# Feed-forward down projection as seven half-size products with weight sums from GpSimd, and a longer matmul time in the recorder's schedule

## The chip, the core and the metric

The kernel runs on one core of a Trainium2 chip. The metric is the device time of one launch in microseconds; three runs of the kernel before gave 1825.97 us as their median (1824.64 to 1826.08).

## What is computed

Two layers of a decoder trunk on 512 tokens of 1024 features, in float32. A layer mixes tokens (convolution, two attentions, gates, an output projection and a layer norm) and then applies a gated feed-forward with a second layer norm. The change lies in the feed-forward and its norm:

```python
def conv_ffn(x, w_up, conv_w, conv_b, w_down):        # w_up 1024 x 5632, w_down 2816 x 1024
    h = causal_dwconv(x @ w_up, conv_w) + conv_b
    a, u = jnp.split(h, 2, axis=-1)
    return (jax.nn.gelu(a, approximate=False) * u) @ w_down
...
x = layer_norm(ALPHA * x + ffn, ln2_g[l], ln2_b[l])
```

## The kernel before

Every float32 product is made of three TensorE matmuls in the replicated-float32 type (F32R): each operand is split into a rounded part (hi, a copy by ScalarE) and the rest (lo, a subtraction by VectorE or GpSimd), and `mm3` adds hi·hi, hi·lo and lo·hi into one PSUM bank. Weights come in units of 128 x 1024 words (512 KB): `unit` issues the load into a `raw` tile on SyncE's queue, makes `wh` on ScalarE and `wl` on VectorE (or GpSimd where `lo=G`). `raw`, `wh` and `wl` have three buffers each. Activations of the feed-forward live in tiles with the tag `big` (eleven buffers).

The up projection has 44 units for a layer (two for each of 22 blocks of 128 hidden features). One unit is 24 matmuls of 512 columns into one of three `mm` banks. `conv_ffn` then takes two banks to one block: an activation and two VectorE operations for each bank, a Gelu, a product `c[0]*c[1]`, and the split of that block into hi and lo (`hb`).

The down projection (`g_tok_norm` with the kind `w_dn`) has tokens on the partitions: for each half n of the 1024 output columns, four token tiles t of 128 have a bank each, and 11 units of two 128-row blocks go by. A unit is 4 x 2 x 3 = 24 matmuls. The last three units of a half are held together so that the token tiles end one after the other; in the second half their lo parts are made on GpSimd. Each ended bank is added to `ALPHA` times the residual (`r`), `bn_stats` follows, and after the second half `g_norm(t)` normalises tile t, writes it out and, in the first layer, transposes and splits it for the next layer. In the last layer the last token tile is done in two matmuls of 256 columns instead of one of 512, so that its first half can be read earlier.

Two clocks set the order. `Sched` runs generators and advances its clock `now` by a matmul time for each matmul and by the waits in the table `DLY`; this is the order of tracing. `Recorder.schedule` then list-schedules all recorded instructions over the five engines with the durations of `Recorder.cost`, an instruction traced earlier going first, and `issue` writes each engine's queue in that order. Both clocks take `n / 2.4 + 3` ns for a matmul of n columns. Each engine runs its queue in order. All instructions carry the line number of one helper (L421 before, L427 after), so that groups are told apart by tile names.

Of the kernel before, what the change touches and what calls it, by code (L numbers as in the profile page):

```python
# [10 lines left out]
F32 = mybir.dt.float32  # L11
# [6 lines left out]
NFF = D_FF // 128  # L18
# [22 lines left out]
def _block(inp, key):  # L41
# [23 lines left out]
    if kind == "w_dn":  # L65
        return _k_block(inp["ffn_w_down"][l], 2 * key[3], 2 * key[3] + 2, key[2] * 512, key[2] * 512 + 512)
# [31 lines left out]
def _smalls(inp, l):  # L98
    """Per-layer constants that sit on partitions: [128, .]"""
# [13 lines left out]
N_UNITS = 290  # L113
# time (ns) that the other engines take until the tensor engine can go on with what a step has made
# [22 lines left out]
def _rearrange(idx, pattern, known):  # L137
    """einops on the free dimensions (the partition dimension p stays first)"""
# [21 lines left out]
class RAP:  # L160
    """an access pattern of a recorded tile: where it lies, and how to get it from the real tile"""
# [45 lines left out]
class Recorder:  # L207
    # ns from the end of an instruction to the start of one that needs it
# [59 lines left out]
    def cost(eng, name, args, kw, op):  # L268
# [34 lines left out]
    def schedule(self):  # L303
        """list scheduling in order of tracing; slots of a tag are given in order of first use"""
# [27 lines left out]
        def slots(op):  # L332
            """None if the slots can be had now, else when (or inf)"""
# [98 lines left out]

class Event:
# [39 lines left out]
def trunk(ctx, tc, xT_d, x_d, w_d, cst_d, sm_d, w1_d, gb_d, out_d, order):  # L473
# [48 lines left out]
    def mm(o, a, b, start, stop):  # L522
        T.matmul(o, a, b, start=start, stop=stop)
# [10 lines left out]
    def mm3(o, ah, al, bh, bl, start, stop):  # L534
        mm(o, ah, bh, start, False)
        mm(o, ah, bl, False, False)
        mm(o, al, bh, False, stop)

# [12 lines left out]
    def unit(*key, parts=1, lo=None):  # L551
# [3 lines left out]
        if key[1] == "n_v":  # L555
            n = 280 * (key[2][1] - key[2][0])
        raw = sb.tile([128, 1024], F32, tag="raw", bufs=3, name=nm("raw"))
# [21 lines left out]
    def g_halves(x, evs, keys):  # L579
        """the first products of a phase, by token halves, as the norm before it delivers them"""  # L580
# [27 lines left out]
    def stack_q(z, a0, a1):  # L608
        """a0 = [hi of rows 0:64; their lo], a1 = [lo of rows 64:128; their hi]"""
# [7 lines left out]
    def stack_k(z, h0, h1, l0, l1):  # L617
        """h0 = [hi; hi] of rows 0:64, h1 of rows 64:128, l0, l1 the same of the lo parts"""
# [6 lines left out]
    def softmax(o, n, mx, sums):  # L625
        """exp((o + causal mask) / 8 - its row maximum), the row sums into sums; mx is left at minus the maximum"""
# [6 lines left out]
    def rsqrt(v, n, r=None, o=None):  # L633
        """(v + eps) ** -0.5"""
# [11 lines left out]
    def g_tok_norm(l, kind, nk, lhs, res_d, gi, last):  # L646
        """norm(ALPHA * x + lhs^T w): the next x (transposed and split, per token tile an event, and in DRAM)"""
        r, st = [], []
        for t in range(4):
# [4 lines left out]
            n = 4 if last and t == 3 else 2  # L654
# [613 lines left out]
```

## Time and profile before

| what | value |
|---|---|
| device time, median of three runs (lowest, highest) | 1825.97 us (1824.64, 1826.08) |
| the profiled execution: span from the first to the last instruction | 1823.5 us |
| PE busy | 1796.3 us (99%) |
| DVE, ACT, POOL busy | 1108.0, 777.7, 216.8 us |
| mean granted TensorE clock | 0.998 |
| mean DMA rate | 106 GB/s |

The profiled execution has no time of its own beside its span; the three runs lie 1.1 to 2.6 us above the span, which is what lies around it. PE, DVE, ACT, POOL and SP are TensorE, VectorE, ScalarE, GpSimd and SyncE. A busy PE is an engine with a matmul in flight; how fast it goes is read from the distance between matmuls. A matmul row names its PSUM tile first, then weights and data. In the page an idle time is that of the engine just before the instruction, with the instruction that ended it.

### The profile page before, as it was taken

The numbers are of one execution on the slowest core, as the hardware profiler recorded it, in microseconds if no ns is written. First come the engines' busy times: TensorE is split into PE (matmuls) and PEld (weight loads), VectorE is DVE, ScalarE is ACT, GpSimd is POOL, SyncE is SP. The second block draws the span as 40 slices with busy tenths as digits, with TensorE's granted clock in tenths as the row PEclk, the third lists the DMA queues.
The fourth block names the chain that finished last, engine by engine and source line by source line (L and its number), as shares of the span: only waits on it lengthen the run. The fifth ranks groups of instructions, "written<-read, shape, count | busy, mean of one in ns | idle before, by whom it ended". The sixth has DMA issues, their size and how long they took to land.

```text
span 1823.5 us, 23236 instructions
## 1 busy us (share of the span) xinstructions
PE 1796.3 (99%) x8794; PEld 1506.6 (83%) x8794; DVE 1108.0 (61%) x1987; ACT 777.7 (43%) x1340; POOL 216.8 (12%) x264
## 2 busy tenths in 40 slices
PE   8999999999999999999999999999999999999997
PEld 7788888888888888888887888888888888888886
DVE  6968968534457566643389688674344666566334
ACT  4548854422324444421244587553223244444211
POOL 1300123000021000000234001120000400000004
PEclk9999999999999999999999999999999999999999
DMA  6520243233234223423254203332333333234221
GB/s 220 153 90 24 60 133 95 91 104 126 96 105 153 100 92 104 139 95 103 93 166 132 76 25 96 101 104 83 108 133 97 123 127 99 98 104 138 94 93 70
DMA packets 60976, 193.36 MB, mean 106 GB/s; under 512 B 7680, under 2 KB 9824, under 8 KB 60736
## 3 DMA queue, kind: packets, MB, share of 16 engines
q1 hardware_dynamic: 49984, 167.01, 27.6%
q0 software_dynamic: 10880, 24.88, 5.4%
q8 instruction: 69, 1.13, 0.3%
q14 instruction: 43, 0.35, 0.1%
HBM read 171.93 MB, written 8.39 MB: 99 GB/s over the span
## 4 chain that ended last, share of the span: by engine, by line
PE 90%; DVE 6%; issue 1%; ACT 1%; POOL 1%; DMA 1%; SPq 0%; POOLq 0%; DVEq 0%; ACTq 0%
PE mm L421 72%; PE sc L421 8%; PE pv L421 6%; DVE tmp L421 4%; PE tp L421 3%; DVE wl L421 1%; DVE s L421 1%; POOL tmp L421 1%; ACT tmp L421 0%; DMA tmp<-in_xT_dram 0%; DVE xl L421 0%; POOL s L421 0%; DVE big L421 0%; ACT big L421 0%; DMA big<-big 0%
## 5 line engine op out<-in xcount | busy, mean ns | idle before, releaser
L421 PE MATMUL mm<-xh,wh 128*128 128x512 f32 (+1 forms) x1632 | 619.9, 381 | 9.0 <-ACT wh L421 5.2
L421 PE MATMUL mm<-xl,wh 128*128 128x512 f32 (+1 forms) x1632 | 619.9, 380 | 3.0 <-DVE xl L421 2.5
L421 PE MATMUL mm<-xh,wl 128*128 128x512 f32 (+1 forms) x1632 | 619.6, 380 | 0.2
L421 DVE TENSOR_TENSOR wl<-raw,wh 128x1024 fp32r<-128x1024 f32 (+2 forms) x270 | 331.8, 1230 | 437.7 <-ACT wh L421 433.6
L421 ACT ACTIVATE wh<-raw 128x1024 fp32r<-128x1024 f32 (+2 forms) x291 | 306.1, 1052 | 523.5 <-PE mm L421 336.4
L421 PEld LDWEIGHTS mm<-xh,wh 128*128 128x128 f32 x1632 | 308.0, 189 | 62.3 <-ACT wh L421 5.2
L421 PEld LDWEIGHTS mm<-xl,wh 128*128 128x128 f32 x1632 | 308.7, 189 | 57.1 <-DVE xl L421 4.5
L421 PEld LDWEIGHTS mm<-xh,wl 128*128 128x128 f32 x1632 | 308.3, 189 | 56.3 <-DVE wl L421 1.3
L421 PE MATMUL mm<-wh,big 128*128 128x512 f32 (+1 forms) x600 | 187.9, 382 | 0.0
L421 ACT ACTIVATE tmp<-tmp,s 128x512 f32<-128x512 f32 (+3 forms) x261 | 140.5, 558 | 63.5 <-DVE s L421 47.0
L421 DVE SCALAR_TENSOR_TENSOR tmp<-mm,smf,tmp 128x511 f32<-128x511 f32 (+1 forms) x176 | 131.3, 746 | 3.1
L421 PEld LDWEIGHTS mm<-wh,big 128*128 128x128 f32 x600 | 111.8, 188 | 21.9
L421 ACT ACTIVATE big<-tmp 128x512 fp32r<-128x512 f32 (+1 forms) x100 | 62.9, 629 | 142.9 <-DVE tmp L421 142.2
L421 PE MATMUL mm<-big,wh 128*128 128x512 f32 x384 | 120.2, 392 | 0.0
L421 PE MATMUL mm<-wl,big 128*128 128x512 f32 (+1 forms) x300 | 114.4, 381 | 0.0
L421 DVE CUSTOM_DVE_ANT_0 tmp<-sc,cst 128x512 f32<-128x512 f32 (+3 forms) x192 | 90.0, 482 | 25.2 <-PE sc L421 24.0
L421 POOL TENSOR_TENSOR wl<-raw,wh 128x1024 fp32r<-128x1024 f32 x21 | 51.5, 2463 | 369.0 <-ACT wh L421 369.0
L421 POOL TENSOR_TENSOR tmp<-tmp,cst 128x512 f32<-128x512 f32 (+1 forms) x46 | 52.0, 1137 | 320.8 <-ACT pt L421 123.6
L421 ACT ACTIVATE tmp<-tmp 128x512 f32<-128x512 f32 (+2 forms) x68 | 41.2, 606 | 113.0 <-DVE tmp L421 112.7
L421 PE MATMUL tp<-cst,tmp 128*128 128x128 f32 x544 | 85.3, 272 | 0.2 <-ACT tmp L421 0.2
L421 PEld LDWEIGHTS mm<-big,wh 128*128 128x128 f32 x384 | 71.6, 188 | 14.6
L421 PE MATMUL sc<-wh,big 128*128 128x512 f32 x240 | 80.5, 390 | 0.0
(145 smaller groups left out, 2070.6 us busy)
## 6 DMA issues: line engine op xcount, KB each, us to landing
raw<-in_w_dram SPq DMA_DIRECT2D x283, 512.0 KB, 3.3
big<-big POOLq DMA_DIRECT2D x48, 128.0 KB, 2.8
res<-tmp SPq DMA_DIRECT2D x24, 256.0 KB, 2.0
tmp<-res POOLq DMA_DIRECT2D x24, 256.0 KB, 3.1
w<-in_w_dram SPq DMA_DIRECT2D x8, 512.0 KB, 5.1
pt<-in_gb_dram POOLq DMA_DIRECT2D x16, 256.0 KB, 4.3
tmp<-tmp POOLq DMA_DIRECT2D x20, 128.0 KB, 2.3
tmp<-in_xT_dram SPq DMA_DIRECT2D x8, 256.0 KB, 7.1
```

What stands on the lines that cost most here:

```text
L421: op.call(*[f(x) for x in op.args], **{k: f(v) for k, v in op.kw.items()})
```

## The change

The feed-forward's hidden block (512 tokens x 2816) is cut into A(i,j): token half i (two tiles of 128), and j for the even or the odd blocks of 128 hidden features. The weights are cut into W(j,n) with n the half of the output columns. Instead of eight products A(i,j)·W(j,n) there are seven, each of two token tiles x 11 blocks x 3 = 66 matmuls of 512 columns, in this order:

| product | left side | weights | ends up in |
|---|---|---|---|
| 1 | A(0,0) | W(0,0) | token half 0, columns 0 |
| 2 | A(0,1) | W(1,0) | token half 0, columns 0 |
| 3 | f = A(1,0)-A(1,1)-A(0,0) | R = W(0,0)+W(0,1)+W(1,1) | bank of 1, then all others |
| 4 | e = A(1,0)-A(1,1) | P = W(0,0)+W(0,1) | both columns 1 |
| 5 | A(0,0)-A(1,0) | Q = W(0,1)+W(1,1) | bank of 3, token half 1 |
| 6 | f + A(0,1) | W(1,1) | bank of 4, token half 0, columns 1 |
| 7 | A(1,1) | Z = R+W(1,0) | bank of 5, token half 1, columns 0 |

`weight_sums(k)` makes P, Q, R, Z for one pair of blocks: two loads of 512 KB, three GpSimd additions (one of 1024 columns, two of 512) and one store of 1 MB to a DRAM tile `sums`, issued on GpSimd's queue; it is called in the up projection after every second block. `loaded` reads the sums back as units. The left sides e, f, A(0,0)-A(1,0) and f+A(0,1) are made on GpSimd, each as five additions of 512 columns and one of 256. The hidden block is kept as plain float32 (`down.h`) and each product's left side is split again by `halves` (ScalarE and VectorE, five of 512 columns and one of 256). The last layer has no 256-column matmuls in this stage any more, all lo parts of these units are on VectorE, and the bias that put the evictions first in the last layer is gone. In both clocks the time of a matmul is `n / 2.4 + 13.6`.

```diff
-                return nb / 2.4 + 3 if nb >= 256 else max(110, nb / 0.6)
+                return nb / 2.4 + 13.6 if nb >= 256 else max(110, nb / 0.6)
...
-            sch.now += n / 2.4 + 3 if n >= 256 else max(107, n / 0.6)
+            sch.now += n / 2.4 + 13.6 if n >= 256 else max(107, n / 0.6)
...
+        def halves(f):
+
+            out = []
+            for m in range(NM):
+                if m % 2 == 0:
+                    c = big(F32R).rearrange("p (m k) (s t) -> p m k s t", m=2, s=2)
+                x = f(m)
+                split(c[:, m % 2, :nks[m], 0], c[:, m % 2, :nks[m], 1], x)
...
+        def sums(op, x, y, to=scratch):
+            def f(m):
+                o = to(m)
+                G.tensor_tensor(o, x(m), y(m), op=op)
+                return o
+            return f
...
+                if u < nu - 2:
+                    group = [(u, ws)]
+                    for i in range(2):
+                        part(x, group, o[i], i, start and u == 0, False, kw)
+                    yield None
+                elif u == nu - 2:
+                    group = [(u, ws)]
+                else:
+                    group.append((u, ws))
+                    for i in range(2):
+                        part(x, group, o[i], i, False, True, kw)
+                        done(i)
+                        yield None
...
+        a, b = [bank("sc"), bank("sc")], [bank("pv"), bank("mm")]
+        x1 = halves(A(0, 0))
+        yield from product(x1, 0, a, True, first_of(0, 0, a, add))
+        x2 = halves(A(0, 1))
+        yield from product(x2, 2, b, True, then_stats(0, 0, more_of(0, 0, b, add)))
+        es, fs = store("xh"), store("xl")
+        e = sums(sub, A(1, 0), A(1, 1), es)
+        f = halves(sums(sub, e, A(0, 0), fs))
+        yield from product(f, R, a, False, first_of(0, 1, a, sub))
+        c = [bank("mm"), bank("mm")]
+        x5 = halves(es)
+        yield from product(x5, P, c, True, first_of(1, 1, c, add))
+        x7 = halves(sums(sub, A(0, 0), A(1, 0)))
+        yield from product(x7, Q, a, False, then_stats(1, 1, more_of(1, 1, a, sub)))
+        x3 = halves(sums(add, fs, A(0, 1)))
+        yield from product(x3, 3, c, False, then_stats(0, 1, more_of(0, 1, c, add), True))
+        x4 = halves(A(1, 1))
+        yield from product(x4, Z, a, False, then_stats(1, 0, first_of(1, 0, a, add), True))
...
-            V.tensor_tensor(c[0], c[0], c[1], op=mult)
-            if i % 2 == 0:
-                hb.append(big(F32R))
-            s = 2 * (i % 2)
-            split(hb[-1][:, s], hb[-1][:, s + 1], c[0])
+            if i % 4 == 0:
+                down.h.append(big())
+            V.tensor_tensor(down.h[-1][:, i % 4], c[0], c[1], op=mult)
+            if i % 2:
+                weight_sums(i // 2)
+
+        def weight_sums(k):
+
+            b, s = big(), big()
+            for j in range(2):
+                order.append((l, "w_dq", k, j))
+                Y.dma_start(b[:, 2 * j:2 * j + 2].rearrange("p a c -> p (a c)"), w_d[len(order) - 1])
+            G.tensor_tensor(s[:, 0:2], b[:, 0:2], b[:, 1:3], op=add)
+            G.tensor_tensor(s[:, 2], s[:, 0], b[:, 2], op=add)
+            G.tensor_tensor(s[:, 3], s[:, 2], b[:, 3], op=add)
+            G.dma_start(down.sums[:, :, k * 512:k * 512 + 512], s)
```

The queues show what moves. **GpSimd's queue at the down projection of the first layer** held, before, the loads of the residual, one small load and the lo parts (`wl`) of the last three units:

```order
L421 DMA tmp_6793<-res_4856 128x512
L421 DMA smf_6800<-in_sm_dram 128x176
L421 TENSOR_TENSOR wl_7281<-raw_7200,wh_7274 128x1024
L421 TENSOR_TENSOR wl_7311<-raw_7230,wh_7304 128x1024
L421 TENSOR_TENSOR wl_7341<-raw_7260,wh_7334 128x1024
```

Now the last weight sum and its store stand at this place, with the residual's loads around them, and then the additions for e (`xh`), f (`xl`) and product 5 (`tmp`) without anything between them; the first of these rows (`big_6750<-big_6709`) is the addition of 1024 columns of the last weight sum, and `big_5196` to `big_6707` are the hidden block:

```order
L427 TENSOR_TENSOR big_6750<-big_6709 128x1024
L427 DMA tmp_6773<-res_4854 128x512
L427 TENSOR_TENSOR big_6750<-big_6750,big_6709 128x512
...
L427 DMA tmp_6883<-res_4854 128x512
L427 TENSOR_TENSOR xh_6892<-big_5196 128x512
L427 TENSOR_TENSOR xh_6892<-big_5487 128x512
L427 TENSOR_TENSOR xl_6909<-xh_6892,big_5196 128x512
...
L427 TENSOR_TENSOR xl_6909<-xh_6892,big_6402 128x512
L427 TENSOR_TENSOR xl_6909<-xh_6892,big_6707 128x256
L427 TENSOR_TENSOR tmp_6999<-big_5196 128x512
```

From `xh_6892<-big_5196` on, 18 additions stand one behind the other (15 of 512 and 3 of 256 columns).

**VectorE's queue behind the end of the up projection of the first layer** held, before, the last operations of `conv_ffn` and then one `wl` after another:

```order
L421 SCALAR_TENSOR_TENSOR tmp_6726<-mm_6683,smf_75,tmp_6726 128x510
L421 TENSOR_TENSOR tmp_6690<-tmp_6690,tmp_6726 128x512
L421 TENSOR_TENSOR big_6676<-tmp_6690,big_6676 128x512
L421 TENSOR_TENSOR wl_6779<-raw_6663,wh_6770 128x1024
L421 TENSOR_TENSOR wl_6815<-raw_6702,wh_6808 128x1024
```

Now the lo parts of the left sides (`big<-big,big`, and `big<-xl,big` for f) stand between the `wl`; the two evictions of product 1 (`tmp<-tmp,sc`) stand ahead of the first `wl` of product 2:

```order
L427 TENSOR_TENSOR wl_6811<-raw_6662,wh_6789 128x1024
L427 TENSOR_TENSOR wl_6821<-raw_6698,wh_6799 128x1024
L427 TENSOR_TENSOR wl_6833<-raw_6738,wh_6818 128x1024
L427 TENSOR_TENSOR big_6828<-big_5196,big_6828 128x2x256
...
L427 TENSOR_TENSOR wl_6873<-raw_6823,wh_6866 128x512
...
L427 SCALAR_TENSOR_TENSOR tmp_6816<-tmp_6816,sc_6778 128x512
L427 TENSOR_TENSOR wl_6912<-raw_6836,wh_6906 128x1024
L427 TENSOR_TENSOR big_6919<-xl_6909,big_6919 128x2x256
L427 TENSOR_TENSOR wl_6933<-raw_6849,wh_6922 128x1024
...
L427 TENSOR_TENSOR wl_7017<-raw_6971,wh_7005 128x512
```

The last row is the `wl` of the last, half-size unit of product 2.

**VectorE's queue at the beginning of product 7 in the first layer**, where token tiles 0 and 1 (`tmp_6773`, `tmp_6796`, `tmp_6816`, `tmp_6840`) are normalised; `wl_7607` and `wl_7645` are the second and the third unit of product 7:

```order
L427 TENSOR_TENSOR tmp_6840<-tmp_6840,mm_7205 128x512
L427 SCALAR_TENSOR_TENSOR tmp_6773<-tmp_6773,s_7563,pt_5029 128x512
...
L427 SCALAR_TENSOR_TENSOR tmp_6796<-tmp_6796,s_7569,pt_5076 128x512
L427 BN_STATS st_7086<-tmp_6840 128x6
L427 TENSOR_TENSOR wl_7607<-raw_7521,wh_7556 128x1024
...
L427 SCALAR_TENSOR_TENSOR tmp_6816<-tmp_6816,s_7619,pt_5029 128x512
...
L427 TENSOR_TENSOR wl_7645<-raw_7526,wh_7572 128x1024
```

Before, all `wl` of the down projection stood ahead of the norms.

## Rows read from the trace of the kernel before

**Rows 1.** The page's head and its part 1: span, busy time of each engine.
```profile
span 1823.5 us, 23236 instructions
PE 1796.3 (99%) x8794; PEld 1506.6 (83%) x8794; DVE 1108.0 (61%) x1987; ACT 777.7 (43%) x1340; POOL 216.8 (12%) x264
```
**Rows 2.** Waits of PE: who, released by whom: us in total, times, longest.
```profile
PE mm L421 <- ACT wh L421: 5.2, 1, 5.2
PE mm L421 <- ACT xh L421: 2.5, 1, 2.5
PE mm L421 <- DVE xl L421: 2.5, 3, 0.8
```
**Rows 3.** Chain of waits, a run of 512-column matmuls: start us, us, what.
```profile
348.99 155.77 PE mm L421 x687
```
**Rows 4.** Chain of waits at the end: matmuls of 256 columns (tp).
```profile
1796.08 0.72 PE tp L421 x6
```
**Rows 5.** Stretches: us, busy (count) of PE, PEld, DVE, ACT, POOL, clock, DMA share, GB/s.
```profile
546.00:786.00 240.00, 239.05 (x1129) 200.77 (x1128) 152.16 (x186) 105.40 (x136) 13.99 (x18) 1.00 0.36 117
786.00:905.50 119.50, 119.50 (x530) 98.93 (x529) 37.59 (x45) 23.15 (x23) 9.66 (x8) 1.00 0.30 98
```
**Rows 6.** Groups by line, first layer's up projection: busy us, mean ns, idle before.
```profile
L421 DVE TENSOR_TENSOR wl<-raw,wh 128x1024 fp32r<-128x1024 f32 x43 | 52.7, 1225 | 70.5 <-ACT wh L421 70.4
L421 ACT ACTIVATE wh<-raw 128x1024 fp32r<-128x1024 f32 x44 | 46.6, 1060 | 27.3 <-PE mm L421 26.2 <-issue 1.0
L421 DVE TENSOR_TENSOR tmp<-tmp,tmp 128x512 f32<-128x512 f32 x21 | 14.5, 691 | 0.7
L421 DVE TENSOR_TENSOR big<-tmp,big 128x512 fp32r<-128x512 f32 x21 | 14.5, 691 | 14.0 <-ACT big L421 14.0
```
**Rows 7.** Groups of POOL, whole program, shapes apart.
```profile
L421 POOL TENSOR_TENSOR wl<-raw,wh 128x1024 fp32r<-128x1024 f32 x21 | 51.5, 2463 | 369.0 <-ACT wh L421 369.0
L421 POOL TENSOR_TENSOR tmp<-tmp,cst 128x512 f32<-128x512 f32 x30 | 39.4, 1314 | 291.6 <-ACT pt L421 123.6 <-DVE tmp L421 89.6 <-DVE s L421 43.2
```
**Rows 8.** Timeline of POOL, 957 to 966 us: start, us, instruction.
```profile
963.59 1.30 POOL L421 TENSOR_TENSOR tmp<-tmp,cst 128x512 f32<-128x512 f32 x1 [2.43 <-DVE tmp L421]
```
**Rows 9.** Timeline of DVE in the same stretch.
```profile
964.00 1.97 DVE L421 TENSOR_TENSOR wl<-raw,wh 128x1024 fp32r<-128x1024 f32 x1
```
**Rows 10.** Timeline of POOL, 913 to 917 us.
```profile
913.82 2.85 POOL L421 TENSOR_TENSOR wl<-raw,wh 128x1024 fp32r<-128x1024 f32 x1
```
**Rows 11.** Timeline of DVE, 911 to 917 us.
```profile
911.82 2.61 DVE L421 SCALAR_TENSOR_TENSOR tmp<-tmp,s,pt 128x512 f32<-128x512 f32 x2
914.36 1.27 DVE L421 TENSOR_TENSOR xl<-tp,xh 128x512 fp32r<-128x512 f32 x2
...
915.97 1.24 DVE L421 SCALAR_TENSOR_TENSOR tmp<-tmp,s,pt 128x512 f32<-128x512 f32 x1
```
**Rows 12.** Timeline of DVE, 900 to 906 us: the norm of two token tiles.
```profile
900.30 2.74 DVE L421 SCALAR_TENSOR_TENSOR tmp<-tmp,s,pt 128x512 f32<-128x512 f32 x4
902.96 0.68 DVE L421 SCALAR_TENSOR_TENSOR tmp<-tmp,pv 128x512 f32<-128x512 f32 x1
903.67 0.69 DVE L421 BATCH_NORM_STATS2 st<-tmp 128x6 f32<-128x512 f32 x1
```
**Rows 13.** Stretches of the start and of the end: columns as in rows 5.
```profile
14.00:16.00 2.00, 2.00 (x13) 2.00 (x13) 1.93 (x4) 1.79 (x5) 0.00 (x0) 1.00 1.08 410
16.00:18.00 2.00, 2.00 (x19) 2.00 (x18) 1.74 (x3) 0.63 (x1) 0.00 (x0) 1.00 0.98 400
1817.00:1818.00 1.00, 0.00 (x0) 0.00 (x0) 1.00 (x2) 0.00 (x0) 0.92 (x3) 0.87 0.56 219
1818.00:1819.00 1.00, 0.00 (x0) 0.00 (x0) 0.54 (x2) 0.00 (x0) 0.86 (x1) 0.50 0.67 262
```
**Rows 14.** Timeline of PE at its end: the last matmul.
```profile
1813.09 0.28 PE L421 MATMUL tp<-wh,big 128*128 128x256 f32 x1
```
**Rows 15.** DMA issues: KB each, median us to landing.
```profile
raw<-in_w_dram SPq DMA_DIRECT2D x283, 512.0 KB, 3.3
```

More of the change, by code (lines that the diff above doesn't have):

```diff
@@ L430, in __getattr__, with __init__ @@
         return lambda *a, **k: self._rec.add(self._eng, name, call, a, k)
+class Down:
+    def __init__(self):
+        self.h, self.sums = [], None
 class Event:
@@ L643, in new_x, with g_down, a_, store @@
                 sb.tile([128, 8, 512], F32R, tag="xl", bufs=1, name=nm("xl")))
+    def g_down(l, src, r, st, nx, g_norm, last):
+        hv = [b.rearrange("p (k j) t -> p k j t", j=2) for b in src.h]
+        NM = len(hv)
+        nks = [2] * (NM - 1) + [1]
+        def a_(i, j, m):
+            return hv[m][:, :nks[m], j, i * 256:i * 256 + 256]
+        def store(tag):
+            f = sb.tile([128, 8, 512], F32, tag=tag, bufs=1, name=nm(tag)).rearrange("p a (k t) -> p a k t", k=2)
+            return lambda m: f[:, m, :nks[m]]
+        def scratch(m):
+            return tmp().rearrange("p (k t) -> p k t", k=2)[:, :nks[m]]
+        def halves(f):
[5 more added lines that the diff above has]
+                split(c[:, m % 2, :nks[m], 0], c[:, m % 2, :nks[m], 1], x)
+                for k in range(nks[m]):
+                    out.append((c[:, m % 2, k, 0], c[:, m % 2, k, 1]))
+            return out
+        def sums(op, x, y, to=scratch):
[4 more added lines that the diff above has]
+            return f
+        def A(i, j):
+            return lambda m: a_(i, j, m)
+        def product(x, w, o, start, done):
+            nu = NM
+            kw = {} if start else dict(skip_group_check=True)
+            for u in range(nu):
+                n = 512 * nks[u]
+                if isinstance(w, int):
+                    ws = unit(l, "w_dn", w, u)
+                else:
+                    ws = loaded(src.sums[:, w[0], u * 1024:u * 1024 + n], n)
+                if u < nu - 2:
[5 more added lines that the diff above has]
+                    group = [(u, ws)]
+                else:
+                    group.append((u, ws))
[3 more added lines that the diff above has]
+                        yield None
+        def part(x, group, o, i, start, stop, kw):
+            ks = [(u, k, ws) for u, ws in group for k in range(nks[u])]
+            for a, (u, k, ws) in enumerate(ks):
+                xh, xl = x[2 * u + k]
+                c = slice(k * 512, k * 512 + 512)
+                mm3(o, xh[:, TOK[i]], xl[:, TOK[i]], ws[0][:, c], ws[1][:, c], start and a == 0, stop and a == len(ks) - 1, **kw)
+        def first_of(half, n, o, op):
+            def f(i):
+                x = r[2 * half + i][n]
+                V.scalar_tensor_tensor(x, x, ALPHA, o[i], op0=mult, op1=op)
+            return f
+        def more_of(half, n, o, op):
+            def f(i):
+                x = r[2 * half + i][n]
+                V.tensor_tensor(x, x, o[i], op=op)
+            return f
+        def then_stats(half, n, f, norm=False):
+            def h(i):
+                f(i)
+                t = 2 * half + i
+                V.bn_stats(st[t][:, n], r[t][n])
+                if norm:
+                    if t == 0 and not last:
+                        nx[0] = new_x()
+                    sch.spawn(0, g_norm(t))
+            return h
+        P, Q, R, Z = ([i] for i in range(4))
+        a, b = [bank("sc"), bank("sc")], [bank("pv"), bank("mm")]
[16 more added lines that the diff above has]
+        yield from product(x4, Z, a, False, then_stats(1, 0, first_of(1, 0, a, add), True))
@@ L653, in g_tok_norm @@
             r.append(rt)
-            n = 4 if last and t == 3 else 2
-            st.append(smp.tile([128, n, 6], F32, tag=f"st{n}", bufs=4 if n == 2 else 1, name=nm("st")))
+            st.append(smp.tile([128, 2, 6], F32, tag="st", bufs=4, name=nm("st")))
         g, b = [pt(), pt()], [pt(), pt()]
@@ L697, in g_norm @@
             sch.set(evs[t], DLY["xsplit"])
+        if kind == "w_dn":
+            yield from g_down(l, lhs, r, st, nx, g_norm, last)
+            return nx[0], evs, res
         nu = nk // 2
@@ L1201, in g_layer @@
             l, "w_o", 8, lambda k: (mh[k // 4][:, k % 4], ml[k // 4][:, k % 4]), res_d, 0, False)
-        hb = []
+        down = Down()
+        down.sums = dp.tile([128, 4, NFF // 2 * 512], F32, tag="sums", bufs=1, name=nm("sums"))
         def conv_ffn(i, oa, ou):
```

68 lines of the change are left out of this document (33 added, 35 removed).

## The prediction

> **What bounds the kernel now.** I read the page's busy times first, then who made PE wait, then the distance between matmuls, and last the stretches. PE is busy for 1796.3 of 1823.5 us [rows 1], and its largest wait is one of 5.2 us at the very start; the next are 2.5 us each [rows 2]. So PE is never short of work for long, and the time is the number of matmuls times their distance. That distance stands in the chain: 687 matmuls in 155.77 us [rows 3], 226.7 ns for 512 columns; for 256 columns 0.72 / 6 = 120 ns [rows 4]. The first layer's down projection has 119.50 us for 528 matmuls, which is 528 x 0.2267 = 119.7 us: no stall at all. VectorE is busy in it for 37.6 us, GpSimd for 9.7 us; in the up projection before it they are at 152.2 and 14.0 of 240 us [rows 5].
>
> The trace's second message is about VectorE and GpSimd together. A GpSimd addition starts at 963.59 and ends at 964.89 [rows 8]; a VectorE `wl` begun at 964.00 ends at 965.97, after 1.97 us [rows 9] where 1.225 us is usual [rows 6]. It ended 1.08 us after GpSimd did: it stood still until then. The other way round, a GpSimd `wl` begun at 913.82 took 2.85 us [rows 10] where the mean is 2.46 us [rows 7]; VectorE ended at 914.43 and GpSimd 2.24 us later [rows 10, 11]. The next VectorE operation (915.97 to 917.21) again ended 0.54 us after GpSimd's end at 916.67. In between, two VectorE operations that read one operand from PSUM took 1.27 us for both, undisturbed [rows 11]. So: VectorE operations with two SBUF operands and GpSimd's two-operand operations exclude each other, one goes after the other by turns, and PSUM readers are free. From the rows a 512-column operation holds the turn for 0.54 us on VectorE, a `wl` for 1.08 us, and a 1024-column one on GpSimd for 2.24 us, so an estimate of 1.12 us for 512 columns and 0.6 us for 256.
>
> **The change part by part.**
>
> *Fewer matmuls.* Each layer does 462 instead of 528 products of 512 columns: 66 x 0.2267 = 15.0 us. In the last layer 132 matmuls of 256 columns had taken the place of 66: 132 x 0.120 = 15.8 us go. Together **-30.8 us**. The Trainium skill (TensorE: Matmul & The Clock Gate, Back-to-back issue gap) gives some 131 ns for a matmul of 512 columns in a sustained stream with weight loads; by that the 132 would be worth 17 us. The run of 687 contradicts it, and the row decides.
>
> *Weight sums in the up projection.* GpSimd gets 11 x (2.46 + 2 x 1.31) = 56 us in a layer [rows 7], VectorE loses 22 lo parts of 0.69 us = 15 us [rows 6]. Even one after the other, 152 - 15 + 14 + 56 = 207 of 240 us: hidden by PE's 240 us, with three `mm` banks and three weight buffers as slack. Loads rise by 512 KB for every unit pair of 10.9 us and the store as much; 117 GB/s would become some 210, while stretches of the start move 400 GB/s [rows 5, 13]. I cost it at nothing; without that cover it would be up to 56 us a layer.
>
> *Products 1 and 2.* This is the term that decides. PE needs 132 x 0.2267 = 29.9 us for them. Between the end of the up projection and the last `wl` of product 2, VectorE's queue holds (from the order): 8 `wl` of full and 2 of half size, 15 lo parts of full and 2 of half size, 1 product `c[0]*c[1]`, and 4 operations on PSUM. GpSimd's queue holds the rest of the last weight sum (half a microsecond and 2 additions) and the 18 additions for e, f and product 5, and f's lo parts, which stand between product 2's `wl`, wait for the additions. Turns held: VectorE 8 x 1.08 + 2 x 0.54 + 15 x 0.54 + 2 x 0.27 + 0.54 = 18.9 us; GpSimd 0.5 + 17 x 1.12 + 3 x 0.6 = 21.3 us. Sum 40.2 us; the four PSUM operations (0.68 us each, [rows 12]) lie beside GpSimd or add up to 2.7 us. After that `wl` 12 matmuls are left, 2.7 us: 42.9 to 45.6 us instead of 29.9. That all 18 additions meet VectorE follows from the turns: only the eight residual loads and the store stand ahead of them on GpSimd, and VectorE has 26 two-operand operations to do in that stretch. From below: if the six additions for product 5 (5 x 1.12 + 0.6 = 6.2 us) fell behind, it would be 6.8 us over instead of 13.0. I take the middle of the full case, **14.4 us a layer, 28.8 us**, bounds 6.8 and 15.7. Nothing at all lost is excluded, since VectorE's queue is never empty there.
> The Trainium skill (SBUF — State Buffer, SBUF: two separate sides) calls this an exclusive lock held for the whole instruction. With whole durations the same instructions give 23.0 + 24.7 = 47.7 us, plus 2.7: some 20 us a layer over instead of 14.4; the rows show the shorter hold, and I go by them.
>
> *Products 3 to 6.* VectorE has 5 x 1.225 + 0.69 for weights, 5 x 0.69 and an estimated 0.4 for the left side and 1.4 to 2.8 us for evictions and `bn_stats` [rows 6, 12]: 12.1 to 13.5 of PE's 15.0 us, so it keeps up. In product 4 the 6.2 us of GpSimd's additions for product 6 come on top: 18.3, 3.3 us too many, but the next products give 1.5 to 2.9 us back each and weights are made up to three units ahead. Bounds 0 and 4 us; I take 1 a layer, **+2**. ScalarE has 5.5 x 1.06 + 5.5 x 0.63 = 9.3 us a product: hidden. Weights come at 512 KB in 2.7 us, 194 GB/s, half of what the start shows [rows 13]; landing takes 3.3 us [rows 15] of the 8.2 us that three buffers give. Nothing.
>
> *Product 7.* In the first layer the norms of tiles 0 and 1 stand between its `wl`: eviction, four operations in 2.74 us, `bn_stats`, `wl` = 0.68 + 2.74 + 0.69 + 1.23 = 5.3 us against 2.7 us of matmuls and 0.9 us of transposes, then two splits from PSUM, four operations and `wl` (1.3 + 2.7 + 1.2 = 5.2) against 3.6 [rows 11, 12]: 1.7 + 1.6 less what starts earlier, **+2.8**. The last layer has fewer of them and no transposes: **+1**. Bounds 0 and 4 each.
>
> *End and transition.* Before, the last matmul starts at 1813.09 and the span ends 10.4 us later [rows 14]. Now token tile 2 ends 9 matmuls (2.0 us) ahead of tile 3, and one chain of eviction, statistics, power and two scalings remains: 0, between -1 and +1.
>
> *The longer matmul time.* 512/2.4 + 13.6 = 226.9 ns agrees with the 226.7 of the rows, so the lists fit the chip better, while the waits in `DLY` now pass in fewer matmuls. All waits of PE outside the start are a few microseconds [rows 1, 2], so little can be gained: 0, between -4 and +5.
>
> **Sum:** -30.8 + 28.8 + 2 + 2.8 + 1 = +3.8 us on the span of 1823.5, which stands 2.5 us below the median; against the median 1825.97 + 3.8 = **1830 us**. What is won in matmuls is paid back as waits for `wl` in products 1 and 2. Its own range, from the bounds that can fall together, is 1822 to 1841.
>
> **The rivals.**
> - *The turns hurt less (faster).* GpSimd reaches its additions late, the six of product 5 fall into products 3 and 4 where VectorE has slack, and each layer loses 6.8 instead of 14.4: 1830 - 15 = **1815**. For it: eight residual loads, whose buffers must be free first, stand ahead of them. Against: GpSimd's additions have no wait between them. It decides from about 12 of 18 additions on. If nothing collided, 1826 - 30.8 + 6 = 1801.
> - *The clock falls (slower).* PE would stand still some 4 to 5 us in one piece before product 1's last unit and again at product 2's first. At the end of the run the granted clock was still full at 1817.0 and at half, 1.2 GHz, by 1818.0, less than 5 us after the last matmul [rows 13, 14]. At the start, before the clock rose, 13 matmuls of 256 columns went in 2 us, then 19 [rows 13]. A fall for some 5 us costs 2.5 us; four of them give **1840**. For it: the size of the stalls; against: they are broken by matmuls in the order. Holding the turn for the whole instruction would lead to the same place, 1842.
> - *The schedule moves elsewhere.* The attentions' order changes with the clock and gains or loses up to 5 us with the sum otherwise as above: **1826**, no difference to see.
> - That the change does not do what it says can be left out: the order shows 66 fewer matmuls of 512 and 132 fewer of 256 columns.
>
> **How the numbers follow.** Forecast 0.48, the faster rival 0.27 (a fifth of it the 1801 case), the slower one 0.15, the last 0.10. Leaving out the 1801 end and the far end of the clock case gives **1807 to 1846**; the likeliest case alone spans 1822 to 1841. About 0.2% (3.7 us, 1822.3 to 1829.6) is what a measurement tells from no change. Faster takes the faster rival and a little of the last, 0.29; the same takes the lower third of the forecast and most of the last, 0.24; slower the rest, 0.47.
>
> **What would show it.** In the profile after: matmuls of product 1 and 2 spread over 43 to 46 us in each layer, with PE waiting for VectorE `wl`; `wl` and the lo parts beside GpSimd's additions at 1.7 to 2.4 us instead of 0.69 and 1.225; products 3 to 6 at about 15 us each; up projections still at 240 us. It is wrong if PE waits less than 7 us in products 1 and 2, if up projections stretch, or if the attentions change by more than 5 us.

## The result, and the profile after

The changed kernel takes **1868.91 us** (median of 4 runs, 1865.6 to 1870.3) against 1825.31 us for the kernel before, measured beside it: a ratio of 1.0237, 95% interval 1.0222 to 1.0251. It is slower by 43.6 us. I had forecast 1830 us with a range up to 1846; slower was the likeliest side, but the size is outside the range.

The page of the changed kernel, head and busy times (against [rows 1]), and PE's waits, by whom they were ended (us in total, times, longest; against [rows 2]):

```profile
span 1866.5 us, 23460 instructions
...
PE 1778.7 (95%) x8596; PEld 1483.6 (79%) x8596; DVE 1256.9 (67%) x2082; ACT 823.0 (44%) x1420; POOL 416.8 (22%) x394
```
```profile
PE sc L427 <- DVE wl L427: 44.3, 7, 23.0
PE tp L427 <- DVE tmp L427: 10.6, 9, 2.7
...
PE pv L427 <- DVE wl L427: 2.9, 2, 1.5
```

PE has the 198 matmuls fewer that were forecast (8794 to 8596), but it waits 44.3 us for VectorE's `wl`, with 23.0 us in one piece, and nine times for VectorE ahead of a transpose, 10.6 us in all. Neither wait is in the list of before. The first is in the down projections. Here is VectorE at the beginning of the first one (start, us, instruction; a wait stands in brackets):

```profile
802.76 0.68 DVE L427 TENSOR_TENSOR big<-tmp,tmp 128x512 f32<-128x512 f32 x1
803.36 20.90 DVE L427 TENSOR_TENSOR big<-big,big 128x256 fp32r<-128x256 f32 x1
824.18 3.48 DVE L427 TENSOR_TENSOR wl<-raw,wh 128x1024 fp32r<-128x1024 f32 x3
```

and GpSimd beside it:

```profile
800.88 2.78 POOL L427 DMA_DIRECT2D tmp<-res  x5
803.56 2.61 POOL L427 TENSOR_TENSOR xh<-big 128x512 f32<-128x512 f32 x2
806.01 2.59 POOL L427 TENSOR_TENSOR xl<-xh,big 128x512 f32<-128x512 f32 x2
...
817.14 6.83 POOL L427 TENSOR_TENSOR tmp<-big 128x512 f32<-128x512 f32 x6
823.90 0.56 POOL L427 DMA_DIRECT2D smf<-in_sm_dram  x1
```

One lo part of 256 columns, 0.4 us of work, took 20.90 us. It ended 0.3 us after the last of the 18 additions, of which the full ones ran undisturbed at 1.22 us each. There were no turns. Three `wl` stood behind it in VectorE's queue, and PE behind those. In the second layer the same thing began, but it ended half way. VectorE first, then GpSimd:

```profile
1730.68 12.45 DVE L427 TENSOR_TENSOR big<-tmp,tmp 128x512 f32<-128x512 f32 x1
...
1743.40 5.63 DVE L427 TENSOR_TENSOR wl<-raw,wh 128x1024 fp32r<-128x1024 f32 x3
1748.95 6.85 DVE L427 TENSOR_TENSOR big<-big,big 128x512 fp32r<-128x512 f32 x4
```
```profile
1731.49 2.60 POOL L427 TENSOR_TENSOR xh<-big 128x512 f32<-128x512 f32 x2
...
1743.22 0.84 POOL L427 TENSOR_TENSOR xh<-big 128x256 f32<-128x256 f32 x1 [0.64 <-DVE big L427]
1744.02 3.93 POOL L427 TENSOR_TENSOR xl<-xh,big 128x512 f32<-128x512 f32 x2
1747.91 10.14 POOL L427 TENSOR_TENSOR tmp<-big 128x512 f32<-128x512 f32 x6
```

The blocked operation was this time the product that GpSimd's tenth addition reads, so GpSimd had to stop for 0.64 us and VectorE got in. From there on the two went by turns, as forecast: four lo parts in 6.85 us are 1.7 us each, which is 0.54 + 1.17.

The stretches (us, then busy time and count of PE, PEld, DVE, ACT, POOL, clock, DMA share, GB/s) of the up projection and of the first blocked piece:

```profile
546.00:786.00 240.00, 237.20 (x1125) 199.24 (x1124) 150.14 (x168) 92.99 (x115) 78.38 (x51) 1.00 0.56 195
...
802.00:826.00 24.00, 0.98 (x3) 0.52 (x3) 24.00 (x6) 3.14 (x5) 22.46 (x23) 0.56 0.30 102
```

The weight sums are in GpSimd's 78.38 us of the up projection, and PE loses nothing to them. (The 2.8 us that it is short of 240 lie at the transition into this stage, below.) In the blocked piece the granted clock is 0.56 of full speed on average: it fell to half, 1.2 GHz, while PE stood still (its last matmul before the wait ends at 802.4, and the clock is at half from 804.8 to 828.7).

By the distance between the starts of matmuls, less 226.9 ns for 512 columns, products 1 and 2 lose 26.0 us in the first layer and 21.3 us in the second to matmuls that start more than 0.3 us late. Matmuls that start less than that late add 1.6 and 3.6 us; most of them stand right behind the long waits, where the clock is at half and matmuls start every 0.43 us.

### The profile page after: what moved, and what is told of

Its sections match the earlier page's. It is cut to its first block, busy times and chain, and to the rows that moved or that the text cites. A ratio compares the mean times of both kernels' runs of the same rounds, so it can differ in the third digit from the quotient of the medians.

```text
span 1866.5 us, 23460 instructions
## 1 busy us (share of the span) xinstructions
PE 1778.7 (95%) x8596; PEld 1483.6 (79%) x8596; DVE 1256.9 (67%) x2082; ACT 823.0 (44%) x1420; POOL 416.8 (22%) x394
## 4 chain that ended last, share of the span: by engine, by line
PE 80%; DVE 11%; issue 6%; ACT 2%; DMA 1%; POOL 1%; SPq 0%; DVEq 0%; ACTq 0%; POOLq 0%
PE mm L427 63%; PE sc L427 9%; DVE tmp L427 5%; PE pv L427 5%; PE tp L427 3%; DVE wl L427 3%; DVE big L427 2%; ACT wh L427 1%; DMA big<-big 1%; DVE s L427 1%; ACT tmp L427 1%; POOL s L427 0%; DMA tmp<-in_xT_dram 0%; ACT big L427 0%; DVE st L427 0%
## 5 line engine op out<-in xcount | busy, mean ns | idle before, releaser
L427 DVE TENSOR_TENSOR wl<-raw,wh 128x1024 fp32r<-128x1024 f32 (+2 forms) x316 | 413.4, 1311 | 403.1 <-ACT wh L427 401.3
L427 ACT ACTIVATE wh<-raw 128x1024 fp32r<-128x1024 f32 (+2 forms) x331 | 341.4, 1034 | 649.1 <-PE mm L427 466.6
L427 PE MATMUL sc<-wh,big 128*128 128x512 f32 x416 | 134.1, 399 | 1.2 <-DVE big L427 1.2
L427 PE MATMUL sc<-wl,big 128*128 128x512 f32 x208 | 84.5, 406 | 44.3 <-DVE wl L427 44.3
L427 POOL TENSOR_TENSOR big<-big 128x1024 f32<-128x1024 f32 x22 | 54.1, 2458 | 321.5 <-DMA big<-in_w_dram 321.5
L427 PE MATMUL mm<-wh,big 128*128 128x512 f32 x380 | 122.4, 391 | 0.0
L427 PEld LDWEIGHTS sc<-wh,big 128*128 128x128 f32 x416 | 80.5, 194 | 18.7 <-DVE big L427 2.0
L427 PE MATMUL tp<-cst,tmp 128*128 128x128 f32 x544 | 84.4, 274 | 10.7 <-DVE tmp L427 10.6
L427 PEld LDWEIGHTS tp<-cst,tmp 128*128 128x128 f32 x544 | 66.5, 141 | 27.6 <-issue 11.8
L427 PEld LDWEIGHTS sc<-wl,big 128*128 128x128 f32 x208 | 40.5, 195 | 55.8 <-DVE wl L427 46.9
```

The source lines that it names most:

```text
L427: op.call(*[f(x) for x in op.args], **{k: f(v) for k, v in op.kw.items()})
```

## The experiments

All ratios are to the kernel before, with 95% intervals. "The sums" are the four left sides e, f, A(0,0)-A(1,0) and f+A(0,1).

**e1_time3: the matmul time back at + 3.**

```diff
-                return nb / 2.4 + 13.6 if nb >= 256 else max(110, nb / 0.6)
+                return nb / 2.4 + 3 if nb >= 256 else max(110, nb / 0.6)
```

> The changed kernel, with the matmul time in both clocks back at n / 2.4 + 3. In its profile the stretch from the first attention to the first matmul of the down projection is 5.9 us longer than before in the first layer and 5.2 us in the second, though nothing was added there but the weight sums. Theory A (the longer matmul time moved the order of the attentions and of the norm between them and the up projection for the worse): those 11 us go, about 1858 us. Theory B (the weight sums on GpSimd cost them): 1869 us, within 3 us, and the two stretches stay long. The loss in the down projections should stay within 5 us either way.

1858.29 us, 1.0180 (1.0165 to 1.0195): 10.6 us less, as theory A said. The waits ahead of transposes fall from 10.6 to 2.1 us, and `wl` still costs 44.0 us.

**e9_before_136: only the longer matmul time, in the kernel before.**

> The kernel of before with the longer matmul time n / 2.4 + 13.6 in both clocks and nothing else. Theory A (the longer time alone sets the attentions' and the norms' order for the worse): 10 to 12 us slower, 1836 us (1834 to 1839), with the same waits of 1 to 3 us in the attentions as in the changed kernel. If the loss needs the new down projection or the weight sums: 1826 us, within 3.

1842.23 us, 1.0091 (1.0076 to 1.0106): 17 us slower, more than expected. The time alone does it, with no new product and no weight sum. PE's waits in this kernel begin with

```profile
PE tp L421 <- DVE tmp L421: 11.0, 8, 2.7
```

and at the step from the attentions to the up projection they look like this, on VectorE and on GpSimd:

```profile
553.15 3.49 DVE L421 SCALAR_TENSOR_TENSOR tmp<-tmp,s,pt 128x512 f32<-128x512 f32 x2 [0.77 <-POOL s L421]
```
```profile
549.72 2.87 POOL L421 TENSOR_TENSOR wl<-raw,wh 128x1024 fp32r<-128x1024 f32 x1
552.54 0.57 POOL L421 TENSOR_TENSOR s<-s,mhalf 128x1 f32<-128x1 f32 x1
553.08 2.35 POOL L421 TENSOR_TENSOR wl<-raw,wh 128x1024 fp32r<-128x1024 f32 x1
```

A transpose stands at the head of PE's queue and waits 2.72 us for the norm, which itself waits for a GpSimd `wl`, while matmuls that could go stand behind it. The number fits the chip's matmuls better and still makes a worse order.

**e2_breaks: a one-column GpSimd operation behind each addition.**

```diff
                 G.tensor_tensor(o, x(m), y(m), op=op)
+                G.tensor_scalar(brk, o[:, 0, 0:1], EPS, None, op0=add)
```

> The changed kernel, with a one-column GpSimd operation on the result behind every left-side addition, so that the 18 additions no longer follow each other without a break. Theory K (VectorE is kept out for as long as two-operand additions of GpSimd follow each other directly, and gets its turn at the first break; that is the 20.90 us VectorE operation of 256 columns): no VectorE operation over 4 us is left in the down projections, the stalls of TensorE in products 1 and 2 fall from 26.0 and 21.3 us to what turns by pairs cost, about 14 us each, and with the clock that does not fall the time is about 1846 us (1838 to 1854). Theory T (what counts is the sum of turns alone, however they are grouped): the stalls stay over 20 us and the time is 1869 us or a little more, for the 24 added operations.

1862.00 us, 1.0202 (1.0186 to 1.0217): only 7 us less, outside both forecasts. VectorE, then GpSimd:

```profile
802.41 7.11 DVE L427 TENSOR_TENSOR big<-big,big 128x256 fp32r<-128x256 f32 x1
809.44 7.22 DVE L427 TENSOR_TENSOR wl<-raw,wh 128x1024 fp32r<-128x1024 f32 x3
```
```profile
805.08 0.33 POOL L427 TENSOR_SCALAR brk<-xh 128x1 f32<-128x1 f32 x1
...
807.73 0.29 POOL L427 TENSOR_SCALAR brk<-xl 128x1 f32<-128x1 f32 x1
...
809.12 0.46 POOL L427 TENSOR_SCALAR brk<-xh 128x1 f32<-128x1 f32 x1
```

Two breaks of 0.3 us let nobody in; at the third VectorE got its turn, and then the engines alternated to the end, a `wl` and an addition in 2.4 us. Products 1 and 2, counted as above, still lose 18.4 and 19.5 us, 7.6 and 1.8 less than in the changed kernel. One VectorE operation of 7.11 us is left in the first layer and one of 7.98 us in the second, so this run does not show what turns alone cost, which I had put at 14.4 us a layer.

**e3_sums_dve: the sums on VectorE.**

```diff
-                G.tensor_tensor(o, x(m), y(m), op=op)
+                V.tensor_tensor(o, x(m), y(m), op=op)
```

> The changed kernel, with the four left-side sums (e, f, A(0,0)-A(1,0), f+A(0,1)) on VectorE instead of GpSimd. The 18 additions of the beginning then cost VectorE some 15 x 0.65 + 3 x 0.4 = 11 us in a layer, and nothing is kept out. Theory K: TensorE's stalls in products 1 and 2 are 5 to 10 us a layer, the clock stays up, about 1834 us (1826 to 1842). Rival L (the loss is VectorE's own longer queue, the lo parts between the wl, whoever makes the sums): the stalls stay at 20 us or grow by the 11 us, 1865 to 1885 us.

1833.78 us, 1.0045 (1.0030 to 1.0060): 35.1 us less, as theory K had it. The edit can reorder all queues, since they are scheduled by list, but the gain lies where the additions stood: products 1 and 2 lose 7.0 and 6.3 us instead of 26.0 and 21.3. PE's waits for `wl` shrink to

```profile
PE sc L427 <- DVE wl L427: 8.9, 8, 2.5
...
PE pv L427 <- DVE wl L427: 4.8, 2, 2.4
```

**e4_no_left_sums: the sums left out.**

> The changed kernel, without the four left-side sums: blocks of the hidden layer stand in their place, so that part of the computation is left out and everything else stays. Theory K and theory T: TensorE's stalls in products 1 and 2 fall to 3 us or less a layer, and the time is 1868.9 - 23 - 18 - 4 (the clock) = about 1822 us (1815 to 1828); the rest over the 1795 us of 30.8 us fewer matmuls is the attentions' 11 us and the norms at product 7. Rival L (VectorE's longer queue alone): over 1850 us.

1832.96 us, 1.0037 (1.0027 to 1.0048): not 1822. Leaving the sums out altogether gains no more than moving them to VectorE, so on VectorE they are all but free, and some 11 us that I had put down to them have another cause: PE still waits 2.7 us in product 1 and 2.2 us at product 2.

**e5_dve_time3: e1 and e3 together.**

> Both edits that helped, together: left-side sums on VectorE, and the matmul time back at n / 2.4 + 3. If the two losses are separate (theory A for the attentions, theory K for products 1 and 2), the gains add: 1868.9 - 10.6 - 35.1 = 1823 us (1819 to 1828), about the time of before. If the longer time only helped to hide something that VectorE's sums now need, it stays over 1830 us.

1823.01 us, 0.9990 (0.9981 to 1.0000). The two gains add. All that was saved in matmuls is still lost elsewhere.

**e6_x1_early: product 1's left side split during the up projection.**

```diff
+            if i % 4 == 3 or i == NFF - 1:
+                first_left(i // 4, 2 if i % 4 == 3 else 1)
```

> The kernel of e5, with the split of product 1's left side A(0,0) made during the up projection, as its blocks come, where VectorE is busy for 150 of 240 us. The remaining stalls of products 1 and 2 (2.7 us in product 1 and 2.6 us at the start of product 2 in each layer, and the clock that falls behind them) are then put down to VectorE's queue at that place: 5.5 lo parts of 0.65 us = 3.6 us a layer less, so the stalls fall to 2 us or less a layer and the time is 1823 - 2 x 4 - 2 = about 1813 us (1807 to 1818). If those stalls come from the loads or from the e and f sums alone, no change: 1823 us. If the eleven buffers run short, the up projection gets longer and it is slower.

1817.72 us, 0.9961 (0.9946 to 0.9976): 5.3 us less, about half of what was expected. PE now waits for ScalarE's `wh` at the start of product 2 (0.8 us in the first layer, 3.1 in the second) and for `wl` behind it, and `wh` for its load. The loads of `raw` in that place (landing time, least, median, most), and the stretch:

```profile
DMA to landing us min/median/max: 3.2/6.9/7.8
```
```profile
795.00:807.00 12.00, 10.61 (x44) 7.63 (x42) 10.90 (x18) 5.61 (x10) 2.79 (x6) 1.00 0.97 355
```

Against 3.3 us in [rows 15] a load takes 6.9, with the DMA engines busy for 97% of the stretch: eight residual loads, the last weight sum and the new units come at once.

**e7_z_third: A(1,1) times Z as third product, in banks of its own, on top of e6.**

> The kernel of e6, with the product A(1,1) times Z done third, in two banks of its own (its result is added to the residual there), and token halves exchanged, so that the half that ends first is again tokens 0 to 255. VectorE gets 15 us more for the sums e and f, and the norm of the first half stands in product W(1,1). If VectorE's queue in products 2 and 3 still bounds e6, 3 to 6 us fewer: about 1808 us (1803 to 1813). If not, the same as e6 within 2 us, since two more evictions (0.69 us each) are added for a layer.

1823.77 us, 0.9994 (0.9984 to 1.0004): 6 us worse than e6. The waits for `wh` stay (2.7 us in the first layer, 4.1 us in the second), so this order was tried while the transfers still bounded the place, and it says little about the order.

**e10_dma_spread: fewer transfers at that place, on top of e6.**

```diff
-            if i % 2:
-                weight_sums(i // 2)
+            for k in [0, 1] if i == 0 else [(i + 3) // 2] if i % 2 and i < NFF - 3 else []:
+                weight_sums(k)
...
+        for t, n in ((0, 1), (1, 1), (2, 1), (3, 1), (2, 0), (3, 0)):
+            G.tensor_scalar(r[t][n][:, 0:1], r[t % 2][0][:, 0:1], EPS, None, op0=add)
+            G.dma_start(r[t][n], res_d[TOK[t], n * 512:n * 512 + 512])
```

> The kernel of e6, with fewer transfers at the beginning of the down projection: the weight sums are made earlier in the up projection (the last one about 35 us before its end instead of at its end), and six of the eight residual loads wait until product 1's tiles have been added up. In e6 TensorE waits some 5 us in the first layer and 3.3 us in the second for ScalarE's wh there, which waits for loads that take 6.9 us instead of 3.3, with the transfers at about 400 GB/s. If that is what bounds this place now: 1817.7 - 8 - 1 to 2 for the clock = about 1808 us (1804 to 1812). If VectorE's queue takes over at once: 1815 us or more.

**1801.92 us**, 0.9873 (0.9858 to 0.9887): faster than both kernels, and a little better than expected. The edit moves the last weight sum's three GpSimd additions away from this place together with its transfers; which part of the gain is whose was not separated. Its page, its waits, and the place that was at 97% in e6:

```profile
span 1799.4 us, 23450 instructions
...
PE 1767.3 (98%) x8596; PEld 1478.0 (82%) x8596; DVE 1239.1 (69%) x2130; ACT 826.1 (46%) x1420; POOL 361.1 (20%) x358
```
```profile
PE mm L427 <- ACT wh L427: 5.5, 1, 5.5
PE sc L427 <- DVE wl L427: 2.9, 3, 1.6
PE tp L427 <- DVE tmp L427: 2.1, 2, 1.8
```
```profile
790.00:802.00 12.00, 12.00 (x55) 9.93 (x54) 11.83 (x18) 5.99 (x9) 0.55 (x1) 1.00 0.48 161
```

Products 1 to 6 have no wait over 0.4 us left; what remains are the norms beside product 7 and the step behind it.

**e14_best_pool_sums: e10 with the sums back on GpSimd.**

> The kernel of e10 with the left-side sums back on GpSimd, the one part undone. Theory K: a wl or lo part of 10 to 13 us beside GpSimd's additions for e and f in each layer, TensorE waits 5 to 9 us for it a layer, the clock falls behind it: 1802 + 14 + 4 = 1820 us (1812 to 1828). If, with product 1's left side made early and the loads spread, the additions are covered: 1800 to 1806 us.

1833.46 us, 1.0039 (1.0026 to 1.0052): 31.5 us more than e10 for one letter in one line, and more than theory K's 18 us, since additions for the later products collide too. PE's waits for `wl` are 21.9 us, the largest 7.0, and VectorE has

```profile
793.13 10.23 DVE L427 TENSOR_TENSOR big<-tmp,tmp 128x512 f32<-128x512 f32 x1
```

**e12_pool_alone: the changed kernel with the transfers of e10, sums still on GpSimd.**

> The changed kernel (sums on GpSimd, longer matmul time), with the transfers taken away from the place: weight sums earlier in the up projection, six of the eight residual loads after product 2, so that GpSimd's additions for e and f no longer stand behind a row of seven DMA issues; the six additions for product 5 come later by themselves. Theory D (a row of DMA issues ahead makes GpSimd run ahead, and only that keeps VectorE out): no VectorE operation over 4 us, stalls of TensorE in products 1 and 2 of 8 to 12 us a layer by turns, 1836 to 1846 us. Theory K (additions that follow each other directly are enough): one VectorE operation of 8 us or more in each layer, and 1843 to 1856 us. Either way it does not reach the 1813 us that e10 plus the 10.6 us of the longer time would give, as long as GpSimd's additions cost VectorE anything.

1847.87 us, 1.0122 (1.0104 to 1.0140). VectorE, then GpSimd:

```profile
798.04 12.13 DVE L427 TENSOR_TENSOR wl<-raw,wh 128x1024 fp32r<-128x1024 f32 x1
```
```profile
796.85 1.13 POOL L427 DMA_DIRECT2D tmp<-res  x2
797.98 1.32 POOL L427 TENSOR_TENSOR xl<-xh,big 128x512 f32<-128x512 f32 x1
...
806.62 2.47 POOL L427 TENSOR_TENSOR xl<-xh,big 128x512 f32<-128x512 f32 x2
810.86 1.64 POOL L427 TENSOR_TENSOR xh<-big 128x256 f32<-128x256 f32 x1 [1.77 <-DVE big L427]
```

Theory D falls: nine additions keep a `wl` out for 12.13 us without a long row of DMA issues ahead of them, until GpSimd has to wait for VectorE. The `wl` ends 1.08 us after the last of the nine (806.62 + 2.47 = 809.09).

**e8_before_18 and e13_before_18_f32: 18 additions at the start of each down projection of the kernel before, whose results nobody reads.** In e8 one operand and the result are of the replicated type, in e13 all are float32.

> The kernel of before, with 18 additions of 512 columns on GpSimd one behind the other at the start of each down projection, whose results nobody reads: the suspected cost by itself. Their run lasts 18 x 1.22 = 22 us. Theory K (kept out until the run ends): one VectorE wl in each down projection lasts 10 to 22 us, and as weights are made two to three units of 5.44 us ahead, TensorE then waits 4 to 11 us a layer: 1834 to 1850 us. Theory T (by turns): no VectorE operation over 2.5 us, TensorE waits for nothing: 1826 us, within 2.

> The kernel of before with 18 additions on GpSimd at the start of each down projection, as in e8, but with plain float32 operands and results, as the sums of the changed kernel have them; in e8 one operand and the result were in the replicated type, and VectorE got in after at most one addition. Theory F (what decides is the form of the additions: float32 ones follow each other without a gap for VectorE): one VectorE wl of 8 us or more in each down projection, and 1826 to 1842 us, as far as weights made ahead cover it. Theory S (what decides is how VectorE comes to it: in e8 its operations arrive one by one, every 5.4 us, and not one behind the other): no VectorE operation over 3 us, 1826 us within 2.

1825.75 us (1.0002, 0.9993 to 1.0012) and 1825.28 us (0.9996, 0.9987 to 1.0006). Neither keeps anything out. In e13, VectorE beside a run of 18:

```profile
812.82 1.81 DVE L421 TENSOR_TENSOR wl<-raw,wh 128x1024 fp32r<-128x1024 f32 x1 [4.17 <-ACT wh L421]
818.26 2.35 DVE L421 TENSOR_TENSOR wl<-raw,wh 128x1024 fp32r<-128x1024 f32 x1 [3.63 <-ACT wh L421]
```

In these two runs a `wl` that comes out of idleness gets in after one addition at most. My theory K, that additions following each other are enough to keep VectorE out, is too simple.

**e15_before_both: e13 with 12 two-operand operations on VectorE as well.**

> The kernel of e13 (before, with 18 float32 additions on GpSimd one behind the other), and on VectorE, beside them, a one-input operation and then 12 subtractions of two float32 operands one behind the other, whose results nobody reads. Theory S (an operation of VectorE that comes directly behind another one, while GpSimd's run is under way, does not get in; one that comes out of idleness does): one VectorE operation of 5 us or more in each down projection, up to the 18 us that GpSimd's run lasts. Theory T (two engines that both have work go by turns): each of the twelve lasts about 1.7 us (0.54 of its own behind 1.16 to 1.2 of GpSimd's), none over 3 us, as in the second half of layer 1's run in the changed kernel. Time 1826 to 1835 us either way; the durations decide.

A single run: 1849.75 us against 1824.66, slower than I expected either way. VectorE, then GpSimd:

```profile
803.97 20.33 DVE L421 TENSOR_TENSOR tmp<-cst,tmp 128x512 f32<-128x512 f32 x12
```
```profile
797.50 30.13 POOL L421 TENSOR_TENSOR tmp<-cst,tmp 128x512 f32<-128x512 f32 x18
```

Twelve operations at 1.70 us: strict turns, nothing kept out, as theory T said, and a wait of 9.0 us for PE in each layer. The first VectorE operation of the run was again a `wl` out of idleness, and the turns held from there on.

**e11_first_lo: e10 with the lo parts of the first three units of a stage on VectorE.**

> The kernel of e10, with the lo parts of a layer's and an up projection's first three units on VectorE instead of GpSimd. In e6 VectorE's norm operations of 0.65 us beside those GpSimd wl last 2.9 us, and TensorE waits 4.0 us in one piece there. If GpSimd's wl keep the norm out: 3 to 5 us fewer than e10. If VectorE is too full there: the same or 2 to 4 us more.

1810.81 us, 0.9920 (0.9903 to 0.9936): 8.9 us worse than e10, where 2 to 4 were the worst expected. PE now waits 7.2 us ahead of transposes for VectorE's `xl` (0.5 us in e10): beside the norms VectorE is too full, and GpSimd's slower `wl` are the better choice there.

## Why the prediction was wrong, point by point

- **Fewer matmuls, -30.8 us: right.** 198 matmuls are gone, and PE's busy time from the kernel before to e10 falls from 1796.3 to 1767.3 us, 29.0.
- **Weight sums at nothing: right.** The up projections go through without a wait of PE.
- **Products 1 and 2, 14.4 us a layer: the step that failed.** I wrote that the two engines "exclude each other, one goes after the other by turns". The exclusion is right, and all 18 additions of the first layer did meet VectorE's queue. But the rows of before that I used show single GpSimd operations, and from those I took the turns. In the changed kernel VectorE was kept out over up to 18 additions at a stretch, and the products lost 26.0 and 21.3 us, 18.5 more than I had for both layers. Breaks in the run (e2) took 9.4 of that away. Moving the sums to VectorE (e3) gives 35.1 us back, their way back in the best kernel (e14) costs 31.5. (VectorE's list in the prediction has 28 two-operand operations, not 26; its sum counts all of them.)
- **The clock: a rival that came beside the forecast, not in its place.** I gave it 1840 us and 0.15. In the down projections the clock fell to half in the three longest waits, of 23.0, 14.8 and 3.1 us. Its price in products 1 and 2 is about 5 us, the 1.6 and 3.6 us of matmuls that start a little late. (The rows that the prediction reads as before and after the clock rose both show a clock of 1.00; only the distance of the matmuls, 0.21 us up to 15.5 us and 0.12 behind, tells them apart.)
- **Products 3 to 6, +2: right** (0.5 us in each layer). **Product 7, +2.8 and +1: right in the first layer (2.4 us); in the second it was 2.3 us instead of 1.**
- **The longer matmul time at nothing, -4 to +5: wrong.** It costs 10.6 us here (e1) and 17 us in the kernel before (e9). I argued that lists which fit the chip better can gain little because PE waits so little; I did not ask what a better number does to waits that had been set with the old one. The text even named it ("the waits in `DLY` now pass in fewer matmuls") and then put it at 0.
- **Transfers at nothing: wrong, but hidden.** In the changed kernel VectorE's blockade was longer. With that gone, loads at the beginning of the down projection bounded the place, and spreading them gave 15.8 us (e6 to e10).

Against the forecast of 1830 us, 38.9 us are missing: 18.5 for the waits of products 1 and 2, 5.2 for the slow matmuls there and 10.6 for the matmul time make 34.3, products 3 to 7 come out as forecast in sum, and 4.6 were not traced.

The account of the 43.6 us by the steps of the experiments, whose sizes depend on the order in which they were taken: -30.8 for matmuls, +10.6 for the matmul time, +35.1 for the sums on GpSimd, +5.3 for product 1's split at a full place, +15.8 for the transfers there, and some 7 that are left in e10 (product 7 and the step behind it): 43.0.

**What stays open** is what decides between being kept out and going by turns. Shown is that neither the type of the additions' operands (e13) nor a long row of DMA issues ahead (e12) decides it alone, and that a wait of GpSimd for VectorE ended it in e12 and in the second layer of the changed kernel. Whether VectorE's operation comes directly behind another one or out of idleness does not decide it: in e12's second layer a `wl` of half size came out of 1.72 us of idleness and was kept out over four additions. VectorE, then GpSimd:

```profile
1760.24 5.86 DVE L427 TENSOR_TENSOR wl<-raw,wh 128x512 fp32r<-128x512 f32 x1 [1.72 <-ACT wh L427]
```
```profile
1760.49 6.20 POOL L427 TENSOR_TENSOR tmp<-big 128x512 f32<-128x512 f32 x5
```

Nor do turns, once begun, always hold as they did in e15. In e1's second layer VectorE had got in at 1732.29, and its next two `wl` still took 10.84 us, where turns take 2.4 us each (e2) and GpSimd waited for nothing:

```profile
1732.29 10.84 DVE L427 TENSOR_TENSOR wl<-raw,wh 128x1024 fp32r<-128x1024 f32 x2
```
```profile
1735.82 7.89 POOL L427 TENSOR_TENSOR tmp<-big 128x512 f32<-128x512 f32 x6
```

One difference was never tested alone. The additions of e8, e13 and e15 read their 512 columns in one piece; those of the left sides read at least one operand in two pieces of 256, a token half of two blocks. In the 17 traces all twelve VectorE operations that were kept out over four additions or more (changed kernel, e1, e2, e12, e14) stand beside additions of two pieces, and beside additions of one piece alone none was kept out over more than two. Two pieces are not enough by themselves, since the turns of the second layer (from 1748.95 on) stand beside such additions too.

## What to carry to other kernels

Before an elementwise operation with two SBUF operands is moved to GpSimd because it is idle, ask what VectorE does at that moment: here an addition took 1.2 us on GpSimd and held up VectorE at least as long, where VectorE itself needs 0.69 us. A queue of such additions without a wait in it can cost more than its sum, so put it where VectorE has slack: there the weight sums, and the 18 additions of e8 and e13, cost nothing. And a constant of a scheduler that was tuned together with others is measured by itself before it is "corrected".

## What the runs showed of the hardware

- VectorE's two-operand operations can stand still behind a run of GpSimd additions for 12.13 us (9 additions) or 20.90 us (18), and GpSimd is not slowed: 1.22 us each. The Trainium skill (SBUF — State Buffer, SBUF: two separate sides) says that whoever starts first has the pair of ports for the whole instruction and the other blocks. The blocking agrees; that it goes on over many instructions is in the runs only. That whoever starts first has it does not show in the recorded starts: in the second layer of the changed kernel VectorE's operation starts at 1730.68 and GpSimd's first addition at 1731.49, and yet the additions went ahead.
- The other way round as well: in e12 a GpSimd addition that wanted to start while VectorE had two-operand operations one behind the other took 3.23 us instead of 1.3.
- Breaks of 0.3 us in GpSimd's run did not let VectorE in twice, and did the third time (e2).
- Turns cost 1.70 us for two operations of 512 columns, 2.4 us for a `wl` and an addition.
